# Key pairs copied by VectorE into a ring of three tiles, and two or three more landing buffers for raw weights, in a two-layer attention backbone

## The chip, the cores and the metric

The kernel runs on one core of a Trainium2 chip. The metric is the time of one execution in device microseconds (us). TensorE is called PE in the profile, its weight loads PEld, VectorE DVE, ScalarE ACT, GpSimd POOL, and SyncE, which here only issues transfers, SP.

## The reference

Two layers work on 512 latent tokens (a grid of 8 rows by 64 columns) and 256 context tokens, 1024 channels wide. Each layer normalises the tokens, modulates them, projects them once with `w_in`, runs two attentions beside each other, gates and projects each, merges them and projects once more. The second layer updates the latent tokens alone. Cut to what matters:

```python
hx = _rmsnorm(x, norm_g) * (1.0 + scale_x) + shift_x          # hc likewise from ctx
px = hx @ w_in
a_k, a_v, b_k, b_v, a_q, b_q, a_z, b_z, g_a, g_b = _split(px, SPLIT_SIZES)
# A: 8 heads of 64, each query sees an 8 x 16 window (learned bias) and all context keys
a_att = _na_latent(qa, ka, va, cka, cva, rpb, rows)
# B: 8 query heads on 2 key/value heads, rotary positions, all latent and context keys
b_att = _gqa_latent(qb, k_all, v_all)
o_a = (a_att * silu(a_z)) @ w_o_a
o_b = (b_att * silu(b_z)) @ w_o_b
merged = sigmoid(g_a) * o_a + sigmoid(g_b) * o_b
x_new = x + gate_x * (merged @ w_out)
# layer 0 does the same for the context tokens with plain attentions among themselves
```

## The kernel before

**Products.** fp32 operands are split into two parts, a rounded one (`hi`) and the rest (`lo`), and each product is three matmuls: hi·hi, lo·hi, hi·lo (`mm3`, lines 460 to 462). A weight of 128 x 512 numbers lands from HBM in a tile named `raw`; ACT makes `whi` from it (lines 430 and 445), and DVE or POOL makes `wlo` as raw minus hi (lines 433 and 447). `raw_tile` hands out the `raw` tiles from a ring of three, so a load can be issued only when the `wlo` of the load three before it is made. `whi` and `wlo` stand in rings of eight.

**Stages of a layer.** Projection of the keys, values and queries of attention A; attention A (called NA below); projection for attention B; attention B (GQA below); merge and output projection. In the profiled execution NA of layer 0 lies from about 140 to 282 us, GQA of layer 0 from 380 to 545, NA of layer 1 from 785 to 895, GQA of layer 1 from 957 to 1066.

**Fill.** While the eight heads of an attention run, PE also works through a list `fill`: gate and output projections, cut into chunks. A chunk is a load of four raw tiles (two for `w_o_a` and `w_o_b`) and the pieces that use them. Between the heads `pipeline` runs a share of the list. Two chunks are loaded ahead of the attention. In NA of layer 1 seven chunks are in the list: two of `C_AZ`, two of `C_BZ`, three gate chunks.

**One NA head.** `na_first` stages the head's keys in a tile `kk` (hi and lo, fp16), `na_scores` makes four blocks of scores (lines 918, 919 and 1006 on PE), DVE adds the bias and takes the row's extreme (line 1009, with the bias tiles `bint` and `bedg`, loaded for each head), ACT takes the exponential (line 1012), DVE or ACT scales it, ACT and POOL split the context part into an fp16 pair `h` (lines 888, 889), and a DMA transpose turns it into `ht` (line 893). `na_values` multiplies `ht` and the window's probabilities with the values (line 1030 and those after it), one head later.

**Staging of keys.** For even heads the keys lie in partitions 0 to 63 and for odd heads in 64 to 127; `kk` needs them in both halves. `stage_k` (line 910) moves them with two DMAs on SP's queue, one for each half, 64 partitions x 2 x 768 fp16. Two fixed `kk` tiles serve even and odd heads. GQA calls `stage_k` twice in each layer, for the two key heads.

**Order.** The program is written as above, but a scheduler then orders each engine's instructions by the times of its own model, with the buffers that the rings have. Each engine, and SP's queue, works in that fixed order: an instruction that waits holds up all that stand behind it. SP's queue carries raw weights, bias tiles, key copies, the spill of gates, and all DMA transposes.

Of the kernel before, what the change touches and what calls it, by code (L numbers as in the profile page):

```python
# [7 lines left out]
F32 = mybir.dt.float32  # L8
F32R = mybir.dt.float32r
BF16 = mybir.dt.bfloat16  # L10
F16 = mybir.dt.float16
# [63 lines left out]
def hybrid_kernel(es: ExitStack, tc, x, ctx, cvec, w_ada, w_ada0, small, gvec, w_in, w_o_a, w_o_b, w_out,  # L75
                  bias_int, bias_edge, rope, ident_d, out):
    nc = tc.nc
    V, S, G, T = nc.vector, nc.scalar, nc.gpsimd, nc.tensor
# [3 lines left out]
    wp = es.enter_context(tc.tile_pool(name="wp", bufs=8))  # L82
# [6 lines left out]
    def nm(s):  # L89
        uid[0] += 1  # L90
        return f"{s}_{uid[0]}"
# [78 lines left out]
    def ada_load(k):  # L170
# [3 lines left out]
        nc.sync.dma_start(w, w_ada0[k])  # L174
        ada_w[k] = w

    def raw_tile():
        return wp.tile([128, 512], F32, tag="raw", name=nm("raw"), bufs=3)

    def load_raw(k):  # L180
        raw0.append(raw_tile())
        nc.sync.dma_start(raw0[k], w_in[0][128 * k:128 * k + 128, C_AK:C_AK + 512])
# [239 lines left out]
    def load_w(src, col0, n, nk, lo_eng, k0=0, own=None, bufs=8):  # L422

        pool, x = (wp, "") if own is None else (own, "x")
        res = []
        for k in range(k0, k0 + nk):
            raw = raw_tile()
            nc.sync.dma_start(raw[:, :n], src[128 * k:128 * k + 128, col0:col0 + n])
            hi = pool.tile([128, 512], F32R, tag="whi" + x, name=nm("whi"), bufs=bufs)
            S.copy(hi[:, :n], raw[:, :n])  # L430
            lo = pool.tile([128, 512], F32R, tag="wlo" + x, name=nm("wlo"), bufs=bufs)
            e = lo_eng(k)
            e.tensor_tensor(lo[:, :n], raw[:, :n], F(hi[:, :n]), ALU.subtract)  # L433
            res.append((hi, lo))
        return res

    def load_w2(src, col0, nk, lo_eng):

        res = []
        for i in range(nk // 2):  # L440
            raw = raw_tile()
            nc.sync.dma_start(raw.rearrange("p (k n) -> p k n", k=2),
                              src[256 * i:256 * i + 256, col0:col0 + 256].rearrange("(k p) n -> p k n", k=2))
            hi = wp.tile([128, 512], F32R, tag="whi", name=nm("whi"), bufs=8)
            S.copy(hi, raw)  # L445
            lo = wp.tile([128, 512], F32R, tag="wlo", name=nm("wlo"), bufs=8)
            lo_eng(i).tensor_tensor(lo, raw, F(hi), ALU.subtract)  # L447
            res += [(hi[:, c:c + 256], lo[:, c:c + 256]) for c in (0, 256)]
        return res
# [178 lines left out]
    def layer(l, hx, nxt, start):  # L628
        first = l == 0
# [19 lines left out]
        att = {}  # L649
# [94 lines left out]
        kav = pairs("ka")  # L744
# [93 lines left out]
        if True:  # L838
# [65 lines left out]
            def rows(a, half):  # L904
                return a[64 * half:64 * half + 64]

            def stage_k(src, j, e, to):

                for half in range(2):
                    nc.sync.dma_start(rows(to, half), rows(src, e)[:, :, j, :])  # L910

            def q_pair(src, e, j):
                return src[:, e, j, :]
# [10 lines left out]
            def ctx_scores(q, kh, kl, ct, late=True):  # L924

                pss = ps_score()
                for i in range(2):
                    scores(pss, q[:, 512 + 128 * i:640 + 128 * i], kh, kl,
                           [(256 * i, 256, cut(512, 768))])
                mx = sp.tile([128, 2], F32, tag="mx", name=nm("mx"), bufs=8)  # L930
                V.tensor_reduce(mx, pss.rearrange("p (i n) -> p i n", i=2), AX, ALU.max, negate=True)
                dq = gq_dq if late else na_dq[:, l:l + 1]
                V.tensor_scalar(mx, mx, dq, P_LOG if late else 0.0, ALU.mult, ALU.add)
                p = p_tile()
                r = sp.tile([128, 2], F32, tag="r", name=nm("r"), bufs=8)
                for i in range(2):
                    S.activation(p[:, 256 * i:256 * i + 256], pss[:, 256 * i:256 * i + 256], AF.Exp,
                                 bias=mx[:, i:i + 1], scale=dq, accum_out=r[:, i:i + 1])
                if not late:
                    softmax_tail(p, 512, r, mx, [(0, 256), (256, 512)])  # L940
                turned(p, 512, ct.rearrange("p a i k n -> p (a i k) n"), G)
                return ct, r
# [20 lines left out]
            def open_att(name, width, n_p, n_t, n_h):  # L963
                st = ExitStack()
                att["p"] = st.enter_context(tc.tile_pool(name=name, bufs=2, reuse_waits="tile"))
                att["w"], att["np"], att["nt"], att["nh"] = width, n_p, n_t, n_h
                att["turn"], att["spare"] = 0, False
                return st


            open_ps(x=1, s=(3, 512), v=(1, 512))
            na_es = open_att(f"na{l}", 512, NP_NA[l], NT_NA, NH_NA)
            bint = att["p"].tile([128, 512], F32, tag="bint", name=nm("bint"), bufs=1)
            bedg = att["p"].tile([128, 512], F32, tag="bedg", name=nm("bedg"), bufs=1)
# [86 lines left out]
                values_of(7, prev)  # L1061
                run(fill, len(fill))

            akt = [att["p"].tile([128, 2, 768], F16, name=nm("kk"), bufs=1) for _ in range(2)]

            def na_first(h):
                j, e = h // 2, h % 2
                kh, kl = akt[e][:, 0], akt[e][:, 1]
                stage_k(kav, j, e, akt[e])
                q = q_pair(qav, e, j)  # L1070
                st = na_scores(h, q, kh, kl)
                if not first:
                    return st, None
                o = 4096 + 1024 * (h % 2)
                ct = turns[:, o:o + 1024].rearrange("p (a i k n) -> p a i k n", a=2, i=2, k=2)
                return st, ctx_scores(q, kh, kl, ct, False)
# [9 lines left out]

            bg = []
            pipeline(fill, 9, na_first, values_of(za, na_values, vsa[:, 1:2], False), bg=bg)


# [77 lines left out]
            for t in range(qt):  # L1168
                tok_proj(w_q, 512, a_hx, t, evac_bq)
                run(bg, 2)  # L1170
                if t == STAGE_T[0]:
                    split_vb()
                if t in STAGE_T:
                    e = STAGE_T.index(t)
                    stage_k(kbv, 0, e, gkt[:, e])

            zb = big("zb")
            for i in range(PRE_GQ * len(spans)):
                run(fill, 1)
                turn_late(1 if i == 0 else 0)  # L1180
            bp_es.close()
            gq_es = open_att(f"gq{l}", 768, NP_GQ[l], 0, NH_GQ[l])
            open_ps(s=(2, 1024), v=(1, 512))
            if first:
# [60 lines left out]
        with tc.tile_pool(name=f"mrg{l}", bufs=1, reuse_waits="tile") as mp:  # L1245
# [3 lines left out]
            for v in range(nv):  # L1249
                src = gd[l][8 * v:8 * v + 8].rearrange("k p -> (k p)").unsqueeze(0)  # L1250
# [236 lines left out]
    def nxt():  # L1487
        if not hx1:
            hx1.extend([[big("hx") for _ in range(2)] for _ in range(2)])
        return hx1  # L1490
    layer(0, hx0, nxt, start)
    layer(1, hx1, None, None)


# [73 lines left out]
```

## Time and profile before

| | |
|---|---|
| time, median of 3 runs | 1138.68 us (1135.82 to 1139.03) |
| the profiled execution's own time | 1141.91 us |
| its span | 1140.0 us |
| mean granted clock of PE | 0.983 |
| busy: PE, DVE, ACT, POOL | 1080.4, 756.2, 608.6, 451.1 us |
| key copies `kk` on SP: number, size, issue to landing | 32, 192 KB, 3.4 us |
| key copies `gk` on SP: number, issue to landing | 8, 2.8 us |
| raw weights of 256 KB from `w_in`: number, issue to landing | 168, 3.1 us |

The profiled execution is 3.2 us longer than the median of the three runs, and its own time is 1.9 us longer than its span. PE is busy nearly all the time, so what counts are the places where PE is idle or slow and who lets it wait there. The busy time of a PE group adds overlapping matmuls, so idle time is read from the stages.

### The profile page before, as it was taken

How to read it: one execution, taken by the hardware profiler on the slowest of the kernel's cores; microseconds unless marked ns; L12 is line 12 of the kernel's file. 1: busy time of each engine (PE TensorE's matmuls, PEld its weight loads, DVE VectorE, ACT ScalarE, POOL GpSimd, SP SyncE). 2: the span in 40 equal slices, each digit the busy share in tenths (PEclk: the TensorE clock that was granted, in tenths of full speed). 3: DMA queues.
4: the chain of work that ended last, by engine and by line, in shares of the span. 5: the costliest groups of instructions: out<-in, count | busy, mean ns of one | idle time of the engine just before them, and what ended most of it. 6: DMA issues, size and time to landing. Idle time of an engine off the chain costs nothing. (4 is left out here: it accounts for less than half of the span.)

```text
span 1140.0 us, 16941 instructions
## 1 busy us (share of the span) xinstructions
PE 1080.4 (95%) x5672; PEld 849.9 (75%) x5672; DVE 756.2 (66%) x1627; ACT 608.6 (53%) x1219; POOL 451.1 (40%) x393
## 2 busy tenths in 40 slices
PE   8999999999999999988999999999987899999998
PEld 5688877788988867665888778887765787666677
DVE  4667978765488577666577775576674675677473
ACT  5455368676333567665230264646685435777431
POOL 1054225455154235374322525332243463564530
PEclk8999999999999999989999999999998999999999
DMA  9555346665553488789433533744566445879742
GB/s 360 199 170 177 90 112 146 155 155 133 176 148 132 122 204 181 162 225 238 158 131 100 188 108 114 232 138 130 121 155 168 131 139 161 194 227 224 199 146 79
DMA packets 249711, 186.08 MB, mean 163 GB/s; under 512 B 160924, under 2 KB 215064, under 8 KB 247960
## 3 DMA queue, kind: packets, MB, share of 16 engines
q1 hardware_dynamic: 242144, 170.47, 55.1%
q0 software_dynamic: 2368, 7.87, 2.1%
q10 hardware_dynamic: 5112, 6.66, 1.9%
q8 instruction: 45, 0.74, 0.3%
q14 instruction: 42, 0.34, 0.1%
HBM read 118.86 MB, written 20.47 MB: 122 GB/s over the span
## 5 line engine op out<-in xcount | busy, mean ns | idle before, releaser
L889 POOL TENSOR_TENSOR h<-p,h 128x256 f16<-128x256 f32 (+2 forms) x104 | 108.5, 1051 | 166.0 <-ACT h L888 127.9
L447 POOL TENSOR_TENSOR wlo<-raw,whi 128x512 fp32r<-128x512 f32 x70 | 96.9, 1387 | 134.6 <-ACT whi L445 108.5
L460 PE MATMUL psf<-hx,whi 128*128 128x512 f32 (+1 forms) x360 | 140.6, 391 | 4.4 <-ACT zt L658 2.2
L462 PE MATMUL psf<-hx,wlo 128*128 128x512 f32 (+1 forms) x360 | 137.9, 383 | 0.0
L461 PE MATMUL psf<-hx,whi 128*128 128x512 f32 (+1 forms) x360 | 137.7, 383 | 0.0
L445 ACT CAST whi<-raw 128x512 fp32r<-128x512 f32 x136 | 83.1, 621 | 79.2 <-DMA raw<-in_w_in_dram 48.7
L461 PE MATMUL psx<-wlo,hx 128*128 128x512 f32 (+1 forms) x328 | 120.8, 369 | 1.3 <-DVE wlo L433 1.3
L460 PE MATMUL psx<-whi,hx 128*128 128x512 f32 (+1 forms) x328 | 121.0, 371 | 0.0
L462 PE MATMUL psx<-whi,hx 128*128 128x512 f32 (+1 forms) x328 | 120.5, 368 | 0.0
L433 POOL TENSOR_TENSOR wlo<-raw,whi 128x512 fp32r<-128x512 f32 x40 | 58.9, 1476 | 125.2 <-ACT whi L430 80.2
L430 ACT CAST whi<-raw 128x512 fp32r<-128x512 f32 x88 | 54.1, 625 | 92.6 <-PE psx L462 31.9
L533 POOL TENSOR_TENSOR ss<-ss,ehalf 128x8 f32<-128x8 f32 (+2 forms) x40 | 63.6, 1595 | 93.0 <-DVE ss L530 88.4
L447 DVE TENSOR_TENSOR wlo<-raw,whi 128x512 fp32r<-128x512 f32 x66 | 70.0, 1063 | 42.2 <-ACT whi L445 41.0
L1199 ACT ACTIVATE p<-pss,mx,vb 128x768 f32<-128x768 f32 x64 | 63.5, 993 | 46.8 <-DVE mx L1198 44.2
L888 ACT CAST h<-p 128x256 f16<-128x256 f32 (+2 forms) x136 | 82.0, 618 | 8.4 <-DMA ht<-h 5.9
L1198 DVE CUSTOM_DVE_ANT_0 p<-pss,vb 128x768 f32<-128x768 f32 x64 | 64.1, 1013 | 28.7 <-PE pss L919 23.9
L460 PEld LDWEIGHTS psf<-hx,whi 128*128 128x128 f32 x360 | 69.4, 193 | 17.6 <-ACT zt L658 3.8
L462 PEld LDWEIGHTS psf<-hx,wlo 128*128 128x128 f32 x360 | 69.1, 192 | 12.3
L461 PEld LDWEIGHTS psf<-hx,whi 128*128 128x128 f32 x360 | 69.2, 192 | 11.2
L460 PE MATMUL psx<-hx,whi 128*128 128x256 f32 (+1 forms) x208 | 70.5, 339 | 6.6 <-ACT whi L445 6.6
L461 PEld LDWEIGHTS psx<-wlo,hx 128*128 128x128 f32 x328 | 62.0, 189 | 12.1 <-DVE wlo L433 2.4
L462 PE MATMUL psx<-hx,wlo 128*128 128x256 f32 (+1 forms) x208 | 69.8, 335 | 0.2 <-POOL wlo L447 0.2
(348 smaller groups left out, 2869.4 us busy)
## 6 DMA issues: line engine op xcount, KB each, us to landing
raw<-in_w_in_dram SPq DMA_DIRECT2D x168, 256.0 KB, 3.1
rawb<-in_w_ada_dram SPq DMA_DIRECT2D x48, 256.0 KB, 2.7
raw<-in_w_out_dram SPq DMA_DIRECT2D x32, 256.0 KB, 3.1
kk<-ka SPq DMA_DIRECT2D x32, 192.0 KB, 3.4
tg<-gs SPq DMA_DIRECT2D x4, 1536.0 KB, 8.2
rawx<-in_w_ada_dram SPq DMA_DIRECT2D x4, 1024.0 KB, 8.5
rawy<-in_w_ada_dram SPq DMA_DIRECT2D x4, 1024.0 KB, 11.1
gs<-zt ACTq DMA_DIRECT2D x16, 256.0 KB, 3.2
```

Of the source, the lines that this page charges most:

```text
L430: S.copy(hi[:, :n], raw[:, :n])
L433: e.tensor_tensor(lo[:, :n], raw[:, :n], F(hi[:, :n]), ALU.subtract)
L445: S.copy(hi, raw)
L447: lo_eng(i).tensor_tensor(lo, raw, F(hi), ALU.subtract)
L460: T.matmul(ps, lhs[0], rhs[0], start=first, stop=False)
L461: T.matmul(ps, lhs[0], rhs[1], start=False, stop=False)
L462: T.matmul(ps, lhs[1], rhs[0], start=False, stop=last)
L533: G.tensor_tensor(ss, ss, ehalf[:, :n], ALU.pow)
L888: S.copy(h[:, 0], p[:, :n])
L889: eng.tensor_tensor(h[:, 1], p[:, :n], h[:, 0], ALU.subtract)
L1198: V.tensor_tensor_reduce(p, pss, lift, gq_ndq, 3e38, ALU.add, ALU.min, mx[:, 0:1])
L1199: S.activation(p, pss, AF.Exp, bias=mx[:, 0:1], scale=gq_dq, accum_out=r[:, i:i + 1])
```

## The change

`stage_k` no longer issues DMAs: VectorE copies the two halves (`V.tensor_copy`, 64 partitions x 1536 fp16 each). The `kk` tiles become a ring of three, one tile for each head, in place of two fixed ones. `raw_tile` gives every second raw tile that is asked for while an attention's pool is open a place in a second ring, `rawp`, in that pool: three tiles in both NA stages and in GQA of layer 0, two in GQA of layer 1. The other raw tiles still come from the ring of three.

```diff
+    more_raw = {"p": None, "n": 0}
+
     def raw_tile():
-        return wp.tile([128, 512], F32, tag="raw", name=nm("raw"), bufs=3)
+        n = 3
+        if more_raw["p"] is not None:
+            more_raw["n"] += 1
+            if more_raw["n"] % 2 == 0:
+                return more_raw["p"].tile([128, 512], F32, tag="rawp", name=nm("raw"), bufs=more_raw["bufs"])
+        return wp.tile([128, 512], F32, tag="raw", name=nm("raw"), bufs=n)
...
                 for half in range(2):
-                    nc.sync.dma_start(rows(to, half), rows(src, e)[:, :, j, :])
+                    V.tensor_copy(rows(to, half), rows(src, e)[:, :, j, :])
...
                 att["turn"], att["spare"] = 0, False
+                more_raw["p"], more_raw["bufs"] = att["p"], 3 if width == 512 or first else 2
+                st.callback(lambda: more_raw.update(p=None))
                 return st
...
-            akt = [att["p"].tile([128, 2, 768], F16, name=nm("kk"), bufs=1) for _ in range(2)]
-
             def na_first(h):
                 j, e = h // 2, h % 2
-                kh, kl = akt[e][:, 0], akt[e][:, 1]
-                stage_k(kav, j, e, akt[e])
+                kk = att["p"].tile([128, 2, 768], F16, tag="kk", name=nm("kk"), bufs=3)
+                kh, kl = kk[:, 0], kk[:, 1]
+                stage_k(kav, j, e, kk)
```

In sum 40 issues leave SP's queue (32 for `kk`, 8 for `gk`) and 40 copies join DVE's. The number of matmuls stays as it is. Since rings and engines differ, the scheduler orders all engines anew from the first attention on. Three places show it; the lines of the program after stand 7 to 9 higher than before, and the numbers in the names are counters that differ a little between the two programs.

SP's queue in NA of layer 1, before. `raw_8972`, `raw_8978`, `raw_8984` and `raw_8990` are the four loads of the last gate chunk; `h_8595` belongs to head 4 (counted from 0), `h_8708` to `h_8754` to head 5, `h_8861` to `h_8907` to head 6.

```order
L893 DMA_TRANSPOSE ht_7946<-h_8595 128x4x128
L893 DMA_TRANSPOSE ht_7946<-h_8708 128x4x64 x2
L893 DMA_TRANSPOSE ht_7946<-h_8724 128x4x128
L893 DMA_TRANSPOSE ht_7946<-h_8739 128x4x128
L893 DMA_TRANSPOSE ht_7946<-h_8754 128x4x128
L893 DMA_TRANSPOSE ht_7946<-h_8861 128x4x64 x2
L893 DMA_TRANSPOSE ht_7946<-h_8877 128x4x128
L893 DMA_TRANSPOSE ht_7946<-h_8892 128x4x128
L662 DMA gs_87<-zt_8969 128x512
L442 DMA raw_8972<-in_w_in_dram 128x2x256
L442 DMA raw_8978<-in_w_in_dram 128x2x256
```

The same queue after. The last gate chunk's loads are `raw_8983`, `raw_8989`, `raw_8995` and `raw_9001` here, and `h_7972` and `h_7988` belong to head 0.

```order
L449 DMA raw_8801<-in_w_in_dram 128x2x256
L449 DMA raw_8807<-in_w_in_dram 128x2x256
L669 DMA zs<-zt_8380 128x512
L449 DMA raw_8813<-in_w_in_dram 128x2x256
L449 DMA raw_8819<-in_w_in_dram 128x2x256
L992 DMA bedg_7947<-b_edge_86 64x128 x2
L449 DMA raw_8983<-in_w_in_dram 128x2x256
L449 DMA raw_8989<-in_w_in_dram 128x2x256
L900 DMA_TRANSPOSE ht_7952<-h_7972 128x4x64 x2
L900 DMA_TRANSPOSE ht_7952<-h_7988 128x4x128
```

The first two loads of that chunk moved from behind ten consecutive transposes of heads 4 to 6 to a place ahead of the stage's first transpose.

DVE at the start of NA of layer 0, before. `qa` is the evacuation of the last turned queries, `za` the evacuation of a fill piece, line 1009 the first two blocks of scores of head 0.

```order
L975 MEMSET bint_1523 128x256
L976 MEMSET bedg_1524 128x256
L977 MEMSET bedg_1524 64x128
L978 MEMSET bedg_1524 64x128
L568 SCALAR_TENSOR_TENSOR qa_1031<-pst_1500,gcol,qa_1031 64x4x128 x2
L660 SCALAR_TENSOR_TENSOR za_778<-za_778,psf_1620 128x512
L447 TENSOR_TENSOR wlo_1684<-raw_1680,whi_1682 128x512
L1009 ISA p_1542,mx_1543<-pss_1537,bedg_1524,ehalf 128x512
```

DVE at the same place after; `kk_1530`, `kk_1697` and `kk_1909` are the keys of heads 0, 1 and 2.

```order
L987 MEMSET bedg_1524 64x128
L917 COPY kk_1530<-ka_161 64x1536 x2
L917 COPY kk_1697<-ka_161 64x1536 x2
L917 COPY kk_1909<-ka_161 64x1536 x2
L575 SCALAR_TENSOR_TENSOR qa_1031<-pst_1500,gcol,qa_1031 64x4x128
L667 SCALAR_TENSOR_TENSOR za_778<-za_778,psf_1619 128x512
L454 TENSOR_TENSOR wlo_1683<-raw_1679,whi_1681 128x512
L1018 ISA p_1541,mx_1542<-pss_1536,bedg_1524,ehalf 128x512
```

Six copies now stand in one block ahead of the evacuations `qa` and `za`; the later heads' copies stand two at a time, a few heads ahead of their use.

ACT near the end of GQA of layer 1, before. Line 1199 is the exponential of a block of scores, `p_10853` and `p_10866` are the first two blocks of the last head, `raw_11033` is a load of `w_o_b`.

```order
L445 CAST whi_11029<-raw_11027 128x512
L1199 ACTIVATE p_10853,r_2206_10847<-pss_10848,mx_10854,vb_9261 128x768
L445 CAST whi_11035<-raw_11033 128x512
L1199 ACTIVATE p_10866,r_2206_10847<-pss_10861,mx_10867,vb_9261 128x768
L888 CAST h_10857<-p_10853 128x768
L445 CAST whi_11077<-raw_11075 128x512
L888 CAST h_10870<-p_10866 128x768
```

ACT at the same place after; the load that was `raw_11033` is `raw_11045` here, and `p_10865` is the last head's first block.

```order
L1207 ACTIVATE p_10865,r_2218_10859<-pss_10860,mx_10866,vb_9273 128x768
L895 CAST h_10869<-p_10865 128x768
L882 COPY ho_10814<-pst_10801 64x512
L1207 ACTIVATE p_10878,r_2218_10859<-pss_10873,mx_10879,vb_9273 128x768
L895 CAST h_10882<-p_10878 128x768
L1207 ACTIVATE p_10891,r_2218_10859<-pss_10886,mx_10892,vb_9273 128x768
L711 CAST gbh_10982<-zb_9821 128x512 x3
L452 CAST whi_11047<-raw_11045 128x512
```

The conversion of that weight moved from between the last head's first two exponentials to behind its third.

## The prediction

> **What bounds the kernel now.** I read the page's busy shares first, then PE's idle time by stage, then the waits in the stage that loses most, and last the events around its longest wait.
>
> ```profile
> PE 1080.4 (95%) x5672; PEld 849.9 (75%) x5672; DVE 756.2 (66%) x1627; ACT 608.6 (53%) x1219; POOL 451.1 (40%) x393
> ...
> core 0: us, PE busy (x) PEld busy (x) DVE busy (x) ACT busy (x) POOL busy (x), PEclk, DMA share, GB/s
> 957.00:1066.00 109.00, 102.78 (x492) 69.31 (x490) 74.84 (x116) 77.27 (x134) 60.99 (x41) 0.98 0.88 215
> 380.00:545.00 165.00, 149.50 (x829) 111.77 (x828) 111.51 (x200) 104.19 (x196) 74.89 (x54) 0.95 0.80 193
> 140.00:282.00 142.00, 136.69 (x837) 111.46 (x836) 103.59 (x307) 99.31 (x231) 65.02 (x73) 0.99 0.59 139
> 785.00:895.00 110.00, 94.99 (x500) 69.19 (x499) 64.83 (x196) 72.80 (x163) 41.84 (x47) 0.97 0.56 138
> ```
>
> PE is the bound: 1080.4 of the span's 1140.0 us. The change leaves its matmuls as they are, so it can only give or take PE's idle time and the time at a lower granted clock. In the four attentions, which the four stage rows show, PE is idle 6.2, 15.5, 5.3 and 15.0 us (length minus busy). NA of layer 1 loses most for its length. Its waits, as engine, what it waited for, us in total, times, longest:
>
> ```profile
> PE psx L460 <- ACT whi L445: 6.6, 2, 6.1
> PE psv L1030 <- DMA ht<-h: 2.0, 2, 1.6
> PE pst L858 <- ACT p L845: 1.8, 2, 1.4
> PE psv L1030 <- ACT h L888: 1.4, 1, 1.4
> ...
> PE psf L460 <- ACT zt L658: 0.9, 1, 0.9
> ...
> ACT whi L445 <- DMA raw<-in_w_in_dram: 13.0, 7, 3.7
> ```
>
> The longest one, followed back in time (start, duration, engine, operation):
>
> ```profile
> 848.27 14.02 SPq L893 DMA_TRANSPOSE ht<-h  x10
> 862.34 0.57 SPq L662 DMA_DIRECT2D gs<-zt  x1
> 863.01 0.94 SPq L442 DMA_DIRECT2D raw<-in_w_in_dram  x2
> ...
> 866.26 1.38 ACT L445 CAST whi<-raw 128x512 fp32r<-128x512 f32 x2 [1.03 <-DMA raw<-in_w_in_dram]
> ...
> 866.93 0.79 PE L460 MATMUL psx<-hx,whi 128*128 128x512 f32 x1 [6.15 <-ACT whi L445]
> ...
> 860.00:880.00 20.00, 13.54 (x52) 10.29 (x52) 7.47 (x16) 8.71 (x17) 7.37 (x6) 0.83 0.70 195
> 865.50:872.00 6.50, 5.07 (x12) 4.01 (x13) 1.17 (x1) 2.43 (x4) 2.56 (x2) 0.50 0.96 268
> ```
>
> The last gate chunk's first load stands on SP's queue behind ten transposes, goes out at 863.01, lands some 3 us later, and PE, which had nothing else left in its order, is idle 6.15 us. Behind that gap the granted clock is 0.50 for 6.5 us: 5.07 us of matmuls that would take about half.
>
> **Term A, the loads in NA of layer 1.** The new order has the first two loads of that chunk ahead of the stage's first transpose, and buffers for them (three `rawp` tiles). The gap goes: 6.15 us, and half of 5.07 at the low clock, 2.5, together −8.7, the value I take. What is late next: the two waits for `ht`, 2.0 us above, if transposes come later. Bounds: −4.1 where the clock still falls and those 2.0 us come twice; −10.7 where they too vanish.
>
> **Term B, the end of GQA of layer 1.** The chain of waits, in order of time:
>
> ```profile
> 1048.12 3.17 DMA raw<-in_w_o_b_dram
> 1051.32 0.63 ACT whi L445
> ...
> 1060.85 0.61 DVE tg L740
> 1061.51 0.50 PE L460 MATMUL psf<-gah,whi 128*128 128x512 f32 x1 [2.57 <-DVE tg L740]
> ```
>
> PE is idle 2.57 us after a chain that a `w_o_b` load begins. The load can go out earlier through the added buffers, though its conversion on ACT now stands behind the last head's third exponential. I take −1.5; ends 0 (the chain keeps its length) and −2.6.
>
> **Term C, other raw weights.** ACT waits 13.0 us for raw weights in NA of layer 1, in seven waits of at most 3.7; most of it PE does not feel. The PE waits there that could hang on ACT being late are `pst`, `psv` on `h` and `psf`: 1.8 + 1.4 + 0.9 = 4.1. I take a quarter, −1.0; ends 0 and −4.1. In the other attentions ACT's waits on raw weights end no PE wait long enough to count, so nothing is taken.
>
> **Term K, the key DMAs.** In the view of the tile `kk`, the time that engines idled until its DMA landed is
>
> ```profile
>   DMA kk<-ka: 0.9, 2
> ```
>
> −0.5 taken, ends 0 and −0.9. The 40 issues leaving SP count in A and C already.
>
> **Term D, the copies.** The trace has no fp16 copy from SBUF to SBUF on DVE. The nearest rows (count, busy us, mean ns):
>
> ```profile
> L375 DVE CAST hx<-half 128x512 fp32r<-128x512 f32 x12 | 5.1, 424 | 12.8 <-ACT half L371 12.8
> L385 DVE TENSOR_SCALAR x<-x,ss 128x512 f32<-128x512 f32 x12 | 5.8, 483 | 7.4 <-POOL ss L388 7.4
> L359 DVE TENSOR_SCALAR y<-xt,ss 128x1024 f32<-128x1024 f32 x6 | 4.5, 746 | 0.5 <-POOL ss L357 0.5
> ...
> L447 DVE TENSOR_TENSOR wlo<-raw,whi x66: 668/694/3998, 99.2 to 1070.6; 128x512 fp32r<-128x512 f32 x66
> ...
> L889 DVE TENSOR_TENSOR h<-p,h x32: 936/959/3606, 384.9 to 1059.9; 128x768 f16<-128x768 f32 x32
> ```
>
> One-operand work takes 0.483 us for 512 and 0.746 for 1024 numbers: 0.51 ns a number and 0.22 us to begin. A copy of 1536 fp16 has the bytes of 768 fp32: 0.22 + 0.39 = 0.61 us by bytes, 1.01 by numbers. From below stands the 0.424 us cast. From above stand the two-operand rows, whose shortest are 668 ns for 512 and 936 for 768: 1.05 ns a number, 1.74 us for 1536. I take 0.61, because a copy has one operand. The Trainium skill ("VectorE: DVE Perf Modes", The perf-mode tier table) gives copies of 16-bit numbers within SBUF four numbers a cycle, 693 ns for 2048; worked out from its parts (150 cycles and 384, at 0.96 GHz), an estimate is 0.56 us, which would leave the sum within 0.4 us; no row here shows it.
>
> Forty copies are 24.4 us on DVE, which idles 1140.0 − 756.2 = 383.8. What counts is where they stand. By the order six stand in a block at the start of NA of layer 0, six at that of layer 1, two a head later, four in each projection for B:
>
> ```profile
> 140.00:160.00 20.00, 17.82 (x108) 15.27 (x107) 17.71 (x41) 8.60 (x17) 4.63 (x3) 1.00 0.44 117
> 180.00:200.00 20.00, 19.73 (x127) 16.12 (x126) 18.65 (x62) 18.48 (x45) 14.02 (x15) 1.00 0.69 157
> 340.00:360.00 20.00, 20.00 (x95) 16.34 (x94) 18.46 (x33) 8.77 (x15) 11.90 (x8) 1.00 0.42 130
> 780.00:800.00 20.00, 20.00 (x97) 14.97 (x96) 12.66 (x36) 12.55 (x28) 7.54 (x8) 1.00 0.47 119
> ```
>
> At 140 to 160 DVE idles 2.29 us and takes 3.66: +1.4, behind which the evacuations `qa` and `za`, the `wlo` and head 0's first scores wait, and PE for those. At 340 to 360 it idles 1.54 and takes 2.44: 0.9 over, of which I count 0.6, since PE has no idle time there. At 780 to 800, 7.34 idle covers 3.66, and at 180 to 200, 1.35 covers a head's 1.22: nothing. Taken +2.0. Below stands 0. At 1.74 us a copy that cover is gone: 10.44 − 2.29, 3.48 − 1.35, 6.96 − 1.54 and 10.44 − 7.34 make 8.1 + 2.1 + 5.4 + 3.1 = +18.7.
>
> **The sum.** −8.7 − 1.5 − 1.0 − 0.5 + 2.0 = −9.7. The profiled execution took 1141.9 us of its own (span 1140.0), so 1132.2; it lay 3.2 above the median 1138.7, so the forecast is 1129.0.
>
> **Rival 1, slower: the copies are dear.** Without D the sum is −11.7. The copy's price decides: at 1.74 us the change costs 18.7 − 11.7 = +7.0, 1145.7. Drawn straight between (0.61, 2.0) and (1.74, 18.7), D eats all gains at about 1.27 us. For it speaks that DVE rows are stretched far beyond their shortest when POOL works:
>
> ```profile
> L447 DVE TENSOR_TENSOR wlo<-raw,whi 128x512 fp32r<-128x512 f32 x66 | 70.0, 1063 | 42.2 <-ACT whi L445 41.0 <-PE psf L462 0.8
> ```
>
> The mean is 1.063 us where the shortest is 0.668, and the longest is 3.998. Against it: the block in NA of layer 0 meets POOL busy only 4.63 of 20 us. The Trainium skill ("SBUF — State Buffer", SBUF: two separate sides) has DVE and GpSimd lock one port pair for a whole instruction, against DVE operations in a two-port mode or with two SBUF inputs; the long `wlo` agree with it, and whether a copy waits so no run here shows. Chance 0.14.
>
> **Rival 2, no change: SP's wait changes its name.** The prefetched loads now stand ahead of the transposes, and SP holds them until a buffer is free.
>
> ```profile
> 793.75 6.53 SPq L893 DMA_TRANSPOSE ht<-h  x5
> ...
> 804.62 1.04 PE L1030 MATMUL psv<-ht,va 128*128 128x512 f16 x4
> ...
> L893 SPq DMA_TRANSPOSE ht<-h x144: 1173/1310/6826, 163.2 to 1065.2; - x144
> ...
> ht<-h SPq DMA_TRANSPOSE x144, 3.2
> ```
>
> From the first transpose's issue at 793.75 to the values at 804.62 are 10.9 us; five transposes of 1.31 and a landing of 3.2 need 9.8. About 1.1 us is spare, and a load that holds SP longer makes PE wait for `ht`. If that returns A, −9.7 + 8.7 = −1.0: 1137.7. Against it: the ring is six deep there. Chance 0.16.
>
> **Rival 3, slower: the new order opens GQA of layer 0.**
>
> ```profile
> PE pss L918 <- ACT p L1199: 6.5, 3, 3.5
> ```
>
> Three waits on the exponential already cost 6.5 us there, in 15.5 us of idle. That stage has no gap that raw buffers close, but is ordered anew. If its idle time doubles, −9.7 + 15.5 = +5.8: 1144.5; it decides from 9.7 us. For it: small shifts in a chain of exponential, `h`, transpose. Against it: the order there keeps its pattern. Chance 0.10.
>
> **Rival 4, more than hoped.** A, B, C and K at their upper ends, D at 0: −10.7 − 2.6 − 4.1 − 0.9 = −18.3, so 1120.4. Chance 0.12.
>
> **How the numbers follow.** The forecast has 0.48, with its own range 1121 to 1135: from near rival 4 up to D grown by 6 us. A measurement of this kernel tells about 0.3%, 3.4 us, from no change: faster is below 1135.3, slower above 1142.1. Forecast and rival 4 are faster, 0.60; rival 2 is the same, 0.16; rivals 1 and 3 are slower, 0.24. For 8 in 10 the range takes in rivals 4 and 2 and the nearer part of 1 and 3: 1119 to 1144.
>
> **What would show it.** A right: no PE gap over 2 us before the last gate chunk in NA of layer 1, and clock 1.00 there. B right: the gap at the end of GQA of layer 1 under 1.5 us. D right: rows of copies near 0.6 us; dear, if their mean is over 1.2 or PE idles more than 4 us at 140 to 160. Rival 2 shows as PE waiting on `ht` at the start of NA of layer 1, rival 3 as more than 20 us of PE idle in GQA of layer 0. The prediction is wrong if A's gap is gone and the time is not below 1135.

## The result and the profile after

The changed kernel takes 1123.14 us, median of 4 runs (1119.77 to 1127.78), against 1138.86 us of the kernel before in the same set (4 runs). The ratio is 0.9872, 95% interval 0.9829 to 0.9915: 9.7 to 19.5 us less. The forecast, 1129.0 within 1119 to 1144, was faster at the right place but too small by 6 us. The profiled execution took 1119.77 us, the shortest of the four, while that of before was among the longest; their spans differ by 22.0 us, the medians by 15.7. What is read below from the two traces overstates the gain by some 40%.

The page's span and its busy shares, after:

```profile
span 1118.0 us, 16953 instructions
...
PE 1073.3 (96%) x5672; PEld 842.5 (75%) x5672; DVE 785.9 (70%) x1667; ACT 607.5 (54%) x1219; POOL 454.3 (41%) x393
```

Of the 22.0 us, PE's idle time gave 14.9 (59.6 before, 44.7 after) and PE's busy time 7.1: the same 5672 matmuls at a mean granted clock of 0.992 instead of 0.983. The stages, by windows (order of columns as before):

```profile
140.00:160.00 20.00, 17.76 (x100) 15.07 (x99) 19.32 (x43) 8.56 (x16) 4.50 (x3) 0.91 0.38 111
320.00:340.00 20.00, 20.00 (x92) 16.05 (x91) 15.87 (x38) 5.19 (x11) 9.36 (x6) 1.00 0.52 155
760.00:780.00 20.00, 19.29 (x89) 15.60 (x88) 16.06 (x26) 10.33 (x20) 4.71 (x3) 1.00 0.36 103
380.00:540.00 160.00, 148.22 (x847) 110.69 (x846) 115.22 (x205) 105.20 (x199) 82.57 (x56) 0.98 0.83 194
781.00:872.00 91.00, 87.06 (x483) 63.45 (x482) 71.80 (x208) 71.92 (x164) 42.60 (x48) 1.00 0.58 139
```

In NA of layer 1, which now lies from 781 to 872, PE idles 3.9 us instead of 15.0, at full clock. GQA of layer 0 (380 to 540) idles 11.8 instead of 15.5, at 0.98 instead of 0.95. PE's longest waits in NA of layer 1, and ACT's wait on raw weights there:

```profile
PE psv L1039 <- issue: 1.3, 1, 1.3
PE psv L1048 <- DVE pt L872: 1.1, 1, 1.1
...
ACT whi L452 <- DMA raw<-in_w_in_dram: 0.6, 1, 0.6
```

The 6.1 us wait for `whi` is gone, and ACT's 13.0 us of waiting on raw weights has come down to 0.6. The copies themselves, as groups on DVE:

```profile
L917 DVE COPY kk<-ka 64x1536 f16<-64x1536 f16 x32 | 22.0, 686 | 0.6
L917 DVE COPY gk<-kb 64x1536 f16<-64x1536 f16 x8 | 4.4, 554 | 0.1
```

26.4 us in all, 0.66 a copy. The blocks stand at 152.2 to 155.7 us, 335.4 to 337.7, 768.8 to 772.7 and 899.8 to 902.1. Two waits tell of GQA. The first row is from GQA of layer 0 (before: 6.5, 3, 3.5), the second from GQA of layer 1, where no such wait stood before:

```profile
PE pss L925 <- ACT p L1207: 0.9, 2, 0.5
...
PE pst L1223 <- DMA ht<-h: 5.3, 3, 2.8
```

### The profile page after: what moved, and what is told of

It is laid out like the page before. It is cut to its first block, busy times and chain, and to the rows that moved or that the text cites. A ratio compares the mean times of both kernels' runs of the same rounds, so it can differ in the third digit from the quotient of the medians.

```text
span 1118.0 us, 16953 instructions
## 1 busy us (share of the span) xinstructions
PE 1073.3 (96%) x5672; PEld 842.5 (75%) x5672; DVE 785.9 (70%) x1667; ACT 607.5 (54%) x1219; POOL 454.3 (41%) x393
## 4 chain that ended last, share of the span: by engine, by line
PE 42%; issue 6%; DVE 6%; DMA 6%; ACT 4%; POOL 2%; SPq 1%; DVEq 0%; POOLq 0%; ACTq 0%
PE psx L468 7%; PE psx L469 7%; PE psx L467 7%; PE psf L467 5%; PE psf L468 4%; PE psf L469 4%; DMA ht<-h 3%; PE pst L1223 1%; PE pst L1224 1%; DMA rawb<-in_w_ada_dram 1%; PE pss L925 1%; PE pss L926 1%; ACT p L1207 1%; ACT h L895 1%; DVE p L1206 1%
## 5 line engine op out<-in xcount | busy, mean ns | idle before, releaser
L454 POOL TENSOR_TENSOR wlo<-raw,whi 128x512 fp32r<-128x512 f32 x70 | 98.5, 1415 | 118.8 <-ACT whi L452 87.6
L440 POOL TENSOR_TENSOR wlo<-raw,whi 128x512 fp32r<-128x512 f32 x40 | 54.4, 1362 | 136.9 <-ACT whi L437 98.4
L469 PEld LDWEIGHTS psx<-whi,hx 128*128 128x128 f32 x328 | 61.9, 189 | 10.1 <-DVE hx L383 0.4
```

The source lines that it names most:

```text
L469: T.matmul(ps, lhs[1], rhs[0], start=False, stop=last)
```

## Experiments

Each kernel is timed against the kernel before on the same chip. The change has three parts: copies in place of transfers, the ring of three `kk` tiles, and raw buffers. The first question was which of them carries the gain.

**1. Copies and ring, no raw buffers.**

```diff
-        if more_raw["p"] is not None:
+        if False:
```

> The change without its raw buffers: VectorE copies the keys into the ring of three kk tiles, every raw weight comes from the ring of three. Buffer theory (the gain comes from raw weights landing earlier; the copies cost about as much as they save): 1138 to 1141 us, ratio to before 0.999 to 1.002, and the PE gap of some 6 us ahead of the last gate chunk in NA of layer 1 is still there. Queue theory (the gain comes from 40 key transfers leaving SP's queue): 1124 to 1129 us, ratio 0.987 to 0.991.

1129.80 us, ratio 0.9934 (0.9908 to 0.9960): between the two ranges, and in neither. The 6 us gap ahead of the last gate chunk is gone without a single added buffer, so term A does not need the buffers. The longest wait of PE in NA of layer 1 is now this:

```profile
PE psv L1039 <- DMA ht<-h: 4.1, 1, 4.1
```

**2. Raw buffers alone.** Before, with `raw_tile` as changed:

```diff
+            if more_raw["n"] % 2 == 0:
+                return more_raw["p"].tile([128, 512], F32, tag="rawp", name=nm("raw"), bufs=more_raw["bufs"])
```

> The raw buffers without the copies: keys are staged by two DMAs into two fixed kk tiles as before. Buffer theory: 1123 to 1128 us, ratio 0.986 to 0.991, the gap in NA of layer 1 gone. Queue theory: 1136 to 1139 us, ratio 0.998 to 1.000, since the loads still share SP's queue with the key transfers.

1135.38 us, ratio 0.9974 (0.9955 to 0.9993). The buffer theory, which was the prediction's, falls. The gap is gone here too, but PE's waits in NA of layer 1 name the keys instead:

```profile
PE pss L925 <- DMA kk<-ka: 4.5, 3, 2.5
```

In NA of layer 0, where before it did not, PE waits for the row's extreme:

```profile
PE pss L1015 <- DVE mx L1018: 4.5, 2, 3.4
```

**3. The change with raw buffers in the NA stages alone.**

```diff
-                more_raw["p"], more_raw["bufs"] = att["p"], 3 if width == 512 or first else 2
+                if width == 512:
+                    more_raw["p"], more_raw["bufs"] = att["p"], 3
```

> The change with raw buffers in the two NA stages alone, none in GQA. If GQA of layer 0, where the trace of after has 10 us less lost than before, owes that to the buffers there: 1130 to 1134 us, ratio 0.992 to 0.996. If it owes it to the copies, to the new order or to differences between executions: as the full change, 1121 to 1126 us, ratio 0.985 to 0.989.

1120.75 us, ratio 0.9851 (0.9827 to 0.9875): nothing is lost without the buffers in GQA. Against experiment 1 it shows what the buffers in NA are worth beside copies and ring: 0.9851 against 0.9934 on the same chip, with intervals apart, some 9 us. In GQA the buffers do something too. PE's wait on the exponential in GQA of layer 0 is back:

```profile
PE pss L925 <- ACT p L1208: 5.5, 3, 3.5
```

and the wait for `ht` in GQA of layer 1 is gone. The pattern holds over all fourteen traces of this case. In the six with buffers in both GQA stages, PE waits 0.9 to 1.0 us on that exponential, and in GQA of layer 1 4.9 to 7.1 us on `ht` and 2.5 to 4.5 us on the exponential; in the eight without, 5.5 to 6.6 us, and in GQA of layer 1 at most 0.5 for either. One of the waits for `ht`, on SP's queue after (start, duration, engine, operation) and on PE, and the landings of the transposes that ended the two longest ones:

```profile
940.09 0.91 SPq L449 DMA_DIRECT2D raw<-in_w_in_dram  x2
941.10 0.49 SPq L449 DMA_DIRECT2D raw<-in_w_o_a_dram  x1
941.89 3.95 SPq L900 DMA_TRANSPOSE ht<-h  x2
...
946.60 0.38 PE L1223 MATMUL pst<-ht,vb 128*128 128x512 f16 x1 [2.36 <-DMA ht<-h]
...
941.89 4.66 DMA ht<-h
1038.62 5.81 DMA ht<-h
```

Three loads of weights stand right ahead of each of these two transposes. They did not hold back the first in the queue, since GpSimd finished its `h` only at 941.86; the second went out 1.3 us after its `h` was done (1037.35). The two took 4.7 and 5.8 us to land, where the median of the 144 transposes is 3.2. That the loads under way made the landings long fits this and is not shown. So in GQA the buffers take away one wait and bring two others, and by the ratios with and without them (0.9872 and 0.9851, intervals overlapping) the whole comes out about even.

**4. Is it the order?** The full change with one memset more at each opening of NA:

```diff
             V.memset(bint[:, 256:512], 0.0)
+            V.memset(bint[:, 256:512], 0.0)
```

> The full change with one memset of 128 x 256 on VectorE done twice at the opening of each NA stage: 0.3 us of work at most twice, but the scheduler moves some 7 per cent of PE's instructions. If the gain belongs to the buffers and copies: 1121 to 1126 us, within 0.3 per cent of the full change. If it is luck of the order: over 1128 us, more than 0.4 per cent from the full change.

1125.03 us, ratio 0.9883 (0.9856 to 0.9909): within 0.2% of the full change, as expected if the gain belongs to the edit. The same question put to the kernel before, with a memset that moves more of its order:

```diff
+            V.memset(big("gk")[:, 0:512], 0.0)
             bint = att["p"].tile([128, 512], F32, tag="bint", name=nm("bint"), bufs=1)
```

> Before, with one memset of 128 x 512 fp32 more on VectorE at the opening of each NA stage; the scheduler moves 683 of PE's some 6230 instructions for it. If orders as such are worth little: 1136 to 1141 us, ratio 0.998 to 1.002. If much of the gain is luck of the order: as far as 8 us or more from before, on either side.

1139.13 us, ratio 1.0003 (0.9986 to 1.0020). The new order keeps the gap:

```profile
PE psx L460 <- ACT whi L445: 5.9, 1, 5.9
```

Two other orders are two samples, no proof; but neither moved the time by more than the uncertainty.

**5. The full change again.** The same file as the change, so there is no edit.

> The full change once more, beside the next three kernels on the same chip, for its place among them: 1120 to 1126 us, ratio 0.984 to 0.990.

1122.60 us, ratio 0.9867 (0.9838 to 0.9895).

**6. The copies' price.** Each copy is done twice:

```diff
                     V.tensor_copy(rows(to, half), rows(src, e)[:, :, j, :])
+                    V.tensor_copy(rows(to, half), rows(src, e)[:, :, j, :])
```

> The full change with every copy of keys done twice over: 40 more copies of 0.55 us (the shortest of the trace after), 22 us more on VectorE. If the copies lie beside other work, as the sum of the prediction had it with 2 us on the path: 0 to 4 us over the full change. If they stand in PE's way wherever they are: 10 us or more over it.

1137.99 us, ratio 1.0003 (0.9984 to 1.0021): 15.4 us over the full change. The second forty copies are not free at all. Two places are seen in the trace. At the start of NA of layer 1, DVE, with PE's wait and the window behind it:

```profile
780.02 5.33 DVE L918 COPY kk<-ka 64x1536 f16<-64x1536 f16 x4
...
779.98 4.37 POOL L454 TENSOR_TENSOR wlo<-raw,whi 128x512 fp32r<-128x512 f32 x3 [15.31 <-ACT whi L452]
...
786.38 0.67 DVE L454 TENSOR_TENSOR wlo<-raw,whi 128x512 fp32r<-128x512 f32 x1
...
PE psx L469 <- DVE wlo L454: 5.9, 1, 5.9
...
785.50:792.50 7.00, 5.39 (x13) 4.28 (x14) 5.72 (x10) 1.55 (x3) 0.00 (x0) 0.51 0.55 153
```

Twelve copies stand there in place of six, and the `wlo` that PE needs comes behind eleven of them. Three of the copies meet a `wlo` of GpSimd and take 1.5 to 1.7 us instead of 0.55, so 3.0 us of the delay come from the meeting and not from the number of copies. PE waits 5.9 us, and the clock stands at 0.51 for the next 7 us: another 2.6 us for 5.39 of matmuls. At the start of NA of layer 0, PE waits for the copies themselves:

```profile
PE pss L926 <- DVE kk L918: 3.7, 1, 3.7
```

There too, two copies meet a `wlo` of GpSimd and take 2.0 us more than alone. The three losses (5.9, 2.6 and 3.7 us) make 12.2 us, against 15.4 between the medians. Of the six copies at the start of NA of layer 1, in the trace after, PE lost no more than 0.71 us (19.29 of 20.00 busy at 760 to 780).

**7. Ring and raw buffers, keys by DMA.**

```diff
-                    V.tensor_copy(rows(to, half), rows(src, e)[:, :, j, :])
+                    nc.sync.dma_start(rows(to, half), rows(src, e)[:, :, j, :])
```

> The ring of three kk tiles and the raw buffers, but the keys staged by DMAs on SP's queue as before. If what helps is that the key transfers leave the queue: 1132 to 1137 us, like raw buffers alone (ratio 0.9974). If it was only that two fixed kk tiles held the next head's keys back (PE waited 3.8 us for kk in the run with raw buffers alone): 1122 to 1127 us.

1135.14 us, ratio 0.9976 (0.9960 to 0.9993), as raw buffers alone: the ring takes nothing off while the transfers stay on the queue. The wait for `kk` that the expectation puts at 3.8 us is 4.5 in the trace of experiment 2.

**8. Copies into two fixed tiles, no raw buffers.** Before, with one line changed:

```diff
-                    nc.sync.dma_start(rows(to, half), rows(src, e)[:, :, j, :])
+                    V.tensor_copy(rows(to, half), rows(src, e)[:, :, j, :])
```

> Copies by VectorE into two fixed kk tiles, no raw buffers: the copies without ring and buffers. If the empty queue is what helps: 1127 to 1132 us, as copies with the ring (ratio 0.9934). If the ring is what helps: 1136 to 1140 us.

1124.60 us, ratio 0.9886 (0.9857 to 0.9916), below both expected ranges. That one line gives what the whole change gives, within the intervals. Beside it the copies with the ring (experiment 1, 0.9934) look slower, and the intervals just overlap. The two traces cannot tell why: experiment 1's profiled execution, 1125.39 us, is the shortest of its six and as long as that of this kernel (1125.72). It stays open. ACT's wait on raw weights in NA of layer 1 is 3.5 us, and PE's longest wait there is the transposes':

```profile
ACT whi L445 <- DMA raw<-in_w_in_dram: 3.5, 2, 1.8
...
PE psv L1030 <- DMA ht<-h: 3.1, 1, 3.1
```

**9. Is it the queue?** Before, with the key transfers on ACT's queue:

```diff
-                    nc.sync.dma_start(rows(to, half), rows(src, e)[:, :, j, :])
+                    nc.scalar.dma_start(rows(to, half), rows(src, e)[:, :, j, :])
```

> Before, with the 40 key transfers issued on ACT's queue in place of SP's: nothing on VectorE, no ring, no buffers. If it is enough that the transfers leave SP's queue: 1123 to 1129 us, as copies into two fixed tiles (ratio 0.9886). If the gain comes from keys that need no transfer and its landing (3.4 us from issue): 1134 to 1141 us.

1132.49 us, ratio 0.9941 (0.9920 to 0.9962): halfway, between the two expected ranges. The transfers take as long as before:

```profile
kk<-ka ACTq DMA_DIRECT2D x32, 192.0 KB, 3.4
```

Leaving SP's queue is worth 6.7 us (4.3 to 9.1), and the big gap closes but for this:

```profile
PE psx L460 <- ACT whi L445: 1.5, 2, 1.0
```

Another 6 us come only with the copy. Whether that is the transfer's landing or the issues' place in ACT's stream, this run does not tell.

**10. Copies into fixed tiles, raw buffers in NA.** Experiment 8 with the edit of experiment 3.

> Copies into two fixed kk tiles, with raw buffers in the two NA stages alone. If copies and buffers add up: 1118 to 1122 us, ratio 0.983 to 0.987, as the full change or with buffers in NA alone (0.9851). If buffers add nothing to the copies: 1123 to 1127 us, as copies into fixed tiles (0.9886).

1124.14 us, ratio 0.9875 (0.9852 to 0.9898), 0.1% below experiment 8: no gain that can be told from none. So the buffers' worth depends on the rest: some 9 us with the ring (experiments 1 and 3), nothing with two fixed tiles.

**11. Half of the copies on ScalarE.** Experiment 3 with this edit:

```diff
-                    V.tensor_copy(rows(to, half), rows(src, e)[:, :, j, :])
+                    (V.tensor_copy if half == 0 else S.copy)(rows(to, half), rows(src, e)[:, :, j, :])
```

> The change with raw buffers in the two NA stages alone and the second half of each pair of keys copied by ScalarE: blocks of three copies on VectorE in place of six. If VectorE's blocks at the start of the NA stages still cost PE 2 to 4 us: 1116 to 1119 us. If ScalarE's copies stand in the way of its exponentials and conversions as much: 1120 to 1126 us.

1119.90 us, ratio 0.9830 (0.9809 to 0.9852), the lowest of all, though its interval overlaps those of the full change and of experiment 3. ScalarE needs more than twice as long for a copy:

```profile
L917 ACT COPY kk<-ka 64x1536 f16<-64x1536 f16 x16 | 23.5, 1470 | 0.4
...
L917 DVE COPY kk<-ka 64x1536 f16<-64x1536 f16 x16 | 10.4, 653 | 0.3
```

and has the time for it. The median falls just on the border between the two expectations, so the experiment does not decide between them. Raw buffers in NA and in GQA of layer 0, but none in GQA of layer 1, which the waits of experiment 3 suggest, was not run.

## Why the prediction was right, and where it was not

**The bound and the place: right.** PE's idle time and its time at half clock were what the change could give, and the longest gap, in NA of layer 1, went.

**Term A: right size, wrong cause.** It promised 8.7 us: 6.15 of idle and 2.5 of half clock. The wait is gone and the clock there is 1.00. The step that failed is the sentence that gave the gap to "buffers for them (three `rawp` tiles)". Copies alone close it (experiments 1 and 8), moving the transfers to another queue closes it (9), and added buffers without the copies close it but leave 4.5 us of waiting for `kk` (2). What they share is that the scheduler places the fill's loads elsewhere: ten transposes in a row ahead of a load stand in that stage of two of the fourteen traces, before and the second kernel of experiment 4, and these two have the gap.

**Term K and "the 40 issues leaving SP count in A and C already": mis-sized.** K was taken as −0.5, at most −0.9, from the time that PE waited for `kk`. The copies into fixed tiles, with nothing else, measured −13 us (ratio 0.9886), of which about half comes with the queue alone and half with the transfer gone. A's gap is part of these 13 us: for A, C, K and D together the forecast has −8.7 − 1.0 − 0.5 + 2.0 = −8.2. The wait that carries the tile's name was a small part of what the transfers on this queue cost. Some 5 of the forecast's missing 6 us lie here; how they spread over A, C and K, the runs do not separate.

**Term C: too small.** ACT's waits on raw weights in NA of layer 1 fell from 13.0 to 0.6 us, where a quarter of the PE waits that could hang on them was taken. Of those on `pst`, `psv` and `psf` in NA of layer 1, 4.1 us before, the trace after has none: the upper end, −4.1, was nearer.

**Term B: wrong.** The end of GQA of layer 1 got no shorter. Its PE waits after:

```profile
PE pst L1223 <- DMA ht<-h: 3.0, 2, 2.8
PE psf L467 <- DVE tg L747: 2.0, 1, 2.0
```

The chain through `tg` waits 2.0 instead of 2.57 us, and the transposes 3.0 more.

**Term D: right in price, and in size as far as the traces show it.** The price taken was 0.61 us; 0.66 is the mean, 0.556 the median. The estimate worked out from the Trainium skill ("VectorE: DVE Perf Modes", The perf-mode tier table) was 0.56 us: the trace agrees for a copy that nothing disturbs. Two windows were misplaced: the blocks stand at 335 and 769 us, ahead of 340 to 360 and 780 to 800. The cover there was about as large; of before:

```profile
320.00:340.00 20.00, 20.00 (x96) 16.18 (x95) 15.84 (x39) 6.56 (x17) 11.57 (x9) 1.00 0.57 162
760.00:780.00 20.00, 20.00 (x96) 16.48 (x95) 12.36 (x28) 9.84 (x17) 5.51 (x4) 1.00 0.44 119
```

DVE idled 4.2 and 7.6 us, and the change cost PE there nothing and 0.7 us. At 140 to 160 PE is 0.06 us less busy than before in the first profile of the change, but 1.7 us less in that of experiment 5, which is the same program:

```profile
140.00:160.00 20.00, 16.11 (x99) 13.73 (x97) 19.32 (x40) 7.64 (x15) 4.33 (x3) 1.00 0.36 103
...
153.23 5.46 DVE L917 COPY kk<-ka 64x1536 f16<-64x1536 f16 x6
...
155.43 2.84 POOL L454 TENSOR_TENSOR wlo<-raw,whi 128x512 fp32r<-128x512 f32 x2 [11.52 <-PE psx L468]
...
160.24 0.72 PE L467 MATMUL psf<-hx,whi 128*128 128x512 f32 x1 [2.00 <-DVE za L667]
```

There a `wlo` of GpSimd starts inside the block, at 155.43; in the first profile it starts at 156.03, just behind it. Two of the six copies take 1.61 and 1.54 us, the block 5.46 us instead of 3.41, and PE waits 2.0 us for the evacuation `za` behind it. The term said +1.4: the cost is there in one execution and not in the other, which the sum did not have. That the cover is thin, experiment 6 shows.

**The rivals.** Rival 1, dear copies, did not come as a whole: the mean of 0.66 us, 0.71 in experiment 5, is far from the 1.27 at which it decides. Its mechanism is real. In the first profile 9 of 40 copies were stretched, none of them in the blocks; in experiment 5 there were 11, two of them in the first block. Rival 2's sign, PE waiting on `ht`, came in GQA of layer 1 (5.3 us) and not in NA of layer 1, where the prediction put it. Rival 3 went the other way: the wait in GQA of layer 0 fell from 6.5 to 0.9 us. The forecast left the buffers' gain there at nothing and their loss in GQA of layer 1 at nothing. The two nearly cancel, which is luck and not foresight.

## What to carry to other kernels

A queue that is worked in order charges a small transfer not only the wait that bears its name but what the loads and transposes behind it lose; the one-line test is to do the copy on an engine with room, before any buffer is added. Here the added buffers took one wait away and brought others, so look for the new wait after adding one. Cover for work put on an engine is counted place by place, and with the other engines at that place: a block of six copies cost PE at most 0.7 us where GpSimd was idle and 2.0 us where a `wlo` of GpSimd fell into it.

## What the runs showed of the hardware

A copy on VectorE and an operation of GpSimd can hold each other up. In the trace after, 31 of the 40 copies take 543 to 559 ns and nine 695 to 1431, and all nine lie beside a GpSimd operation on 128 x 256 numbers or more. The longest pair, on DVE, and on POOL at the same time:

```profile
187.09 2.57 DVE L917 COPY kk<-ka 64x1536 f16<-64x1536 f16 x2
...
185.24 2.56 POOL L454 TENSOR_TENSOR wlo<-raw,whi 128x512 fp32r<-128x512 f32 x2 [0.98 <-ACT whi L452]
187.75 1.49 POOL L896 TENSOR_TENSOR hc<-p,hc 128x512 f16<-128x512 f32 x1
```

It goes the other way too, where the copy has begun first: at 808.78 two copies keep their pace and POOL's `h`, 0.68 us just before, takes 0.89:

```profile
808.78 1.13 DVE L917 COPY kk<-ka 64x1536 f16<-64x1536 f16 x2
...
808.21 0.68 POOL L896 TENSOR_TENSOR h<-p,h 128x256 f16<-128x256 f32 x1 [0.33 <-ACT h L895]
809.56 0.89 POOL L896 TENSOR_TENSOR h<-p,h 128x256 f16<-128x256 f32 x1 [0.67 <-ACT h L895]
```

The Trainium skill ("SBUF — State Buffer", SBUF: two separate sides) has the one that starts first keep a shared port pair for its whole instruction; the trace agrees in these places, and shows it for a copy with a single operand. It does not show it everywhere: the eight copies for `gk` start within the span of a GpSimd operation on 128 x 8 numbers (at 334.21 for 3.5 us and at 899.74 for 1.8 us) and keep 543 to 558 ns.
